# Second down projection of a two-layer decoder: 512 weight columns per matmul in three of four accumulator banks

## The chip, the cores and the metric

The kernel runs on one core of a Trainium2 chip. Its engines are named in the profile as PE (TensorE, the matmuls), PEld (the weight loads of TensorE), DVE (VectorE), ACT (ScalarE), POOL (GpSimd) and SP (SyncE, which issues most of the DMAs). The metric is the device time of one execution in microseconds (us); lower is better. The table below gives the median of three runs.

## The reference

The reference is a decoder trunk of two layers for 256 tokens of 1024 features, all in float32. A layer is a mixer (a gated short convolution in the first layer, causal attention in the second) and a channel mixer, and a last norm follows. The part that matters here is the channel mixer of the second layer and the norm behind it:

```python
def conv_glu_ffn(h, w_up, conv_w, conv_b, w_down):
    u = causal_dwconv(h @ w_up, conv_w) + conv_b
    g, v = jnp.split(u, 2, axis=-1)
    return (jax.nn.silu(g) * v) @ w_down
...
x = x + conv_glu_ffn(rms_norm(x, f_norm[layer]), f_w_up[layer], f_conv[layer],
                     f_conv_b[layer], f_w_down[layer])
return rms_norm(x, final_norm)
```

The hidden size of the channel mixer is 2816, so `w_up` is 1024 x 5632 and `w_down` is 2816 x 1024.

## The kernel before

**Products in three parts.** TensorE works on the type float32r. To keep float32's precision, each operand is split into a high part (written by ScalarE as float32r) and a low part (the rest, by VectorE), and a product is the sum of three matmuls: high by high, high by low, low by high. `mm3` (lines 168 to 171) and `token_bank` (lines 190 to 203) issue these three into the same place of PSUM.

**Units.** The weights come in units, in two sizes. A unit of the big tag B is 128 x 2048 (one block of 128 hidden features of `w_up`, gate and value), a unit of the small tag S is 128 x 1024 (128 rows of `w_down`, for instance). Each tag has three slots. For a unit, SyncE loads the raw tile (`load`), ScalarE makes the high part (`split_hi`, line 91), VectorE the low part (`split_lo`, line 97). A unit knows its place in the list of its tag, `u.at` (line 70). In the S list stand 8 units of `w_mb`, 8 of `w_mo`, 22 of the first `w_down`, 8 of `w_o` and then the 22 of the second `w_down`, `DN[1]`, whose places are therefore 46 to 67. A slot's raw tile is loaded anew when its low part has been made (lines 116 and 117); its high part is rewritten when the unit that held the slot has been marked used.

**The channel mixer.** `ffn` runs over 22 blocks of hidden features, by hand in program order (the schedule is manual: each engine executes its instructions in the order in which they are written). For block i it issues `up_step` (48 matmuls: 8 feature tiles, gate and value, 3 products, each 256 columns for the 256 tokens; the weights of the unit are the stationary operand), `conv` (VectorE and ScalarE: scale, convolution over three tokens; it also calls for the next B splits), `gate` (ScalarE's silu, VectorE's product, then the hidden block split into `sh` and `sl`), and, three blocks behind, the down projection of block i - 3 (`down_step`, lines 205 to 209). The last three down units follow behind the loop in `token_last` (lines 220 to 231), in an order by bank, so that the sums, the norm and the output of one bank can run beside the products of the next.

**The second down projection.** In the second layer, `down_step` calls `token_bank`: there the hidden block is the stationary operand (128 hidden features by 128 tokens, taken from `sh` and `sl`) and the weights of the unit stream by as columns. The result is 256 tokens by 1024 features, in four PSUM banks of 128 tokens by 512 features: bank b has tokens `b // 2` and features `b % 2`. Each bank is filled in two halves of 256 columns (`HALVES`, line 55). Bank 3 has its second half in a bank of its own, `acc[4]` (the tile named misc in the profile), which the end of the kernel needs. One `down_step` is thus 4 banks x 2 halves x 3 products = 24 matmuls of 256 columns, and it adds to what the earlier units have left in the banks; only the first unit's first matmul into a bank has `start`.

**Places in memory.** Many tiles are made wider than needed and start at an offset (64 or 48 elements, for instance lines 84, 139 and 251 to 253). `Rows` (lines 247 to 256) holds the normed input of a stage as 8 tiles of 256 tokens and, in `again`, a second copy of the first one, which stands at 32 elements where the eight stand at 48 + 256 and on. Steps called with `again=True` read this copy for their tile 0; in the second `ffn` these are the steps of blocks 1, 2 and 6.

Of the kernel before, what the change touches and what calls it, by code (L numbers as in the profile page):

```python
# [42 lines left out]
def yoco_kernel(ctx: ExitStack, tc: tile.TileContext, t: dict, out: bass.AP):  # L43
    nc = tc.nc
    V, A, G, PE = nc.vector, nc.scalar, nc.gpsimd, nc.tensor
# [97 lines left out]
    first = const.tile([128, 1], F32, name="first")  # L143
# [43 lines left out]
            mm3(acc[b][:, m % 2, :], u.hi[:, m * 128:(m + 1) * 128], u.lo[:, m * 128:(m + 1) * 128],  # L187
                hh, hl, start=(first and m % 2 == 0), stop=last)

    def token_bank(u, b, acc, hh, hl, first, last, c=slice(0, 512)):  # L190


        tok, f0 = slice(b // 2 * 128, b // 2 * 128 + 128), b % 2 * 512
        for d in HALVES:
            if not c.start <= d.start < c.stop:
                continue
            apart = b == 3 and d.start > 0
            o = acc[4 if apart else b].rearrange("p a s -> p (a s)")[:, d]
            f = slice(f0 + d.start, f0 + d.stop)
            PE.matmul(o, hh[:, tok], u.hi[:, f], start=(first and (apart or d.start == 0)), stop=False,  # L200
                      skip_group_check=True)
            PE.matmul(o, hh[:, tok], u.lo[:, f], start=False, stop=False, skip_group_check=True)  # L202
            PE.matmul(o, hl[:, tok], u.hi[:, f], start=False, stop=last, skip_group_check=True)  # L203
# [16 lines left out]
    def token_last(us, acc, hs):  # L220

        for u in us:
            assert u.lo is not None
        for n, u in enumerate(us):
            for b in (0, 1):
                token_bank(u, b, acc, *hs[n], False, n == len(us) - 1)
        for b, c in ((2, slice(0, 512)), (3, HALVES[0]), (3, HALVES[1])):
            for n, u in enumerate(us):
                token_bank(u, b, acc, *hs[n], False, n == len(us) - 1, c)
        for u in us:  # L230
            u.used = True

    def acc_bank():
        return psum.tile([128, 2, S], F32, name="acc", bufs=4)
# [193 lines left out]
    def mixer_a(j, fill=None):  # L428

        w = [par(P_CONV, 3 * j + n) for n in range(3)]  # L430
        m = tmp.tile([128, 2, S], F32, name="u", bufs=2)
        V.tensor_mul(m[:, 1, :], mc[j][:, 0, :], rr[:, 1, :])
        V.tensor_mul(m[:, 0, :], mc[j][:, 1, :], m[:, 1, :])
        o = tmp.tile([128, 2, S], F32, name="cv", bufs=2)
        A.activation(o[:, 0, :], m[:, 0, :], AF.Identity, scale=w[2])
        hi("B")
        if fill:
            lo(fill)
        tap(o[:, 0, :], m[:, 0, :], w[1], 1)
        tap(o[:, 0, :], m[:, 0, :], w[0], 2)  # L440
        V.tensor_mul(o[:, 1, :], o[:, 0, :], rr[:, 0, :])
        return o[:, 1, :]
# [33 lines left out]
    for i in range(2):  # L476
        o = mixer_a(i, "B")
# [8 lines left out]
    o = mixer_a(3, "B")  # L486
    hi("S")
    mixer_b(3, o, "S")
    acc = [acc_bank() for _ in range(4)]
# [4 lines left out]
    for j in range(4, KT):  # L494
        mc[j] = up_bank()
        up_step(MC[j], mc[j], xh, xl, 2)
        o = mixer_a(j, "S")
# [19 lines left out]
    def ffn(layer, xh, xl, sq, bank=down_bank, between=None):  # L517
# [79 lines left out]
        if bank is token_bank:  # L597
            token_last(dn[FJ - 3:], acc, [hd[j] for j in range(FJ - 3, FJ)])
        else:
            down_step(dn[FJ - 3], acc, hd[FJ - 3])  # L600
            down_last(dn[FJ - 2:], acc, [hd[FJ - 2], hd[FJ - 1]])
# [3 lines left out]
    acc = ffn(0, xh, xl, sq)  # L605
# [274 lines left out]
    acc = [acc_bank() for _ in range(4)]  # L880
# [24 lines left out]
    def turn(n):  # L905
# [5 lines left out]
        V.transpose(dst[:, :, :, 32 * a:32 * a + 32], src)  # L911

    acc = ffn(1, xh, xl, sq, token_bank, turn)


# [102 lines left out]
```

## Time and profile before

| | us |
|---|---|
| median of 3 runs (lowest, highest) | 568.54 (568.38, 568.77) |
| span of the profiled execution | 566.6 |
| busy: PEld / DVE / ACT | 554.1 / 472.9 / 341.7 |
| second up and down projections, first to last matmul | 379.9 to 560.5 |

A profiled execution is one run; its span reaches from the first to the last instruction, and what the runs count beyond it is launch and end. In the timeline rows that follow, the columns are the start (us from the span's start), the duration (us), the engine, the line of the kernel, the operation, the tiles (out<-in) and the shape (rows * columns of the stationary operand, then rows x streamed columns), and xN counts merged neighbours. TensorE's matmuls overlap in these rows, each being shown until its last result is written; what one costs is read from start to start.

### The profile page before, as it was taken

How to read it: one execution, taken by the hardware profiler on the slowest of the kernel's cores; microseconds unless marked ns; L12 is line 12 of the kernel's file. 1: busy time of each engine (PE TensorE's matmuls, PEld its weight loads, DVE VectorE, ACT ScalarE, POOL GpSimd, SP SyncE). 2: the span in 40 equal slices, each digit the busy share in tenths (PEclk: the TensorE clock that was granted, in tenths of full speed). 3: DMA queues.
4: the chain of work that ended last, by engine and by line, in shares of the span. 5: the costliest groups of instructions: out<-in, count | busy, mean ns of one | idle time of the engine just before them, and what ended most of it. 6: DMA issues, size and time to landing. Idle time of an engine off the chain costs nothing.

```text
span 566.6 us, 11823 instructions
## 1 busy us (share of the span) xinstructions
PE 558.4 (99%) x4908; PEld 554.1 (98%) x4908; DVE 472.9 (83%) x817; ACT 341.7 (60%) x525; POOL 10.4 (2%) x32
## 2 busy tenths in 40 slices
PE   8999999999999999999999999999999999999995
PEld 8999999999999999999999999999999999999995
DVE  5998869899877787787897999858999888889876
ACT  7765437567654665466756777656676556546534
POOL 0400000000000000000000000000000000000001
PEclk9999999999999999999999999999999999999998
DMA  8986583447556545655265565644656554563211
GB/s 294 387 300 220 181 299 120 149 152 243 193 197 224 186 160 213 223 175 197 75 214 168 202 206 216 195 178 150 223 186 223 223 193 159 208 222 117 72 38 75
DMA packets 24181, 108.48 MB, mean 191 GB/s; under 512 B 2736, under 2 KB 5440, under 8 KB 16192
## 3 DMA queue, kind: packets, MB, share of 16 engines
q1 hardware_dynamic: 23840, 107.43, 52.9%
q8 instruction: 38, 0.62, 0.4%
q10 hardware_dynamic: 288, 0.30, 0.1%
q14 instruction: 15, 0.12, 0.1%
HBM read 106.65 MB, written 1.07 MB: 190 GB/s over the span
## 4 chain that ended last, share of the span: by engine, by line
PE 97%; DMA 1%; ACT 1%; issue 0%; DVE 0%; SPq 0%; POOLq 0%; POOL 0%; ACTq 0%
PE up L171 20%; PE up L169 20%; PE up L170 20%; PE acc L169 7%; PE acc L171 7%; PE acc L170 7%; PE acc L203 3%; PE acc L200 3%; PE acc L202 3%; PE up L757 1%; PE acc L627 1%; PE acc L629 1%; PE acc L630 1%; DMA xres<-xT 1%; PE acc L682 1%; PE misc L203 0%
## 5 line engine op out<-in xcount | busy, mean ns | idle before, releaser
L169 PE MATMUL up<-xh,hiB 128*128 128x256 f32 x944 | 261.4, 277 | 0.8 <-ACT hiB L91 0.8
L171 PE MATMUL up<-xh,loB 128*128 128x256 f32 x944 | 261.1, 277 | 0.3 <-DVE loB L97 0.2
L170 PE MATMUL up<-xl,hiB 128*128 128x256 f32 x944 | 260.8, 276 | 0.0
L169 PEld LDWEIGHTS up<-xh,hiB 128*128 128x128 f32 x944 | 177.2, 188 | 1.5 <-ACT hiB L91 1.0
L171 PEld LDWEIGHTS up<-xh,loB 128*128 128x128 f32 x944 | 177.2, 188 | 0.7 <-DVE loB L97 0.7
L170 PEld LDWEIGHTS up<-xl,hiB 128*128 128x128 f32 x944 | 177.3, 188 | 0.0
L97 DVE TENSOR_TENSOR loB<-rawB,hiB 128x2048 fp32r<-128x2048 f32 (+2 forms) x76 | 147.8, 1948 | 3.7 <-ACT hiB L91 3.5
L91 ACT ACTIVATE hiB<-rawB 128x2048 fp32r<-128x2048 f32 (+1 forms) x73 | 123.6, 1697 | 15.2 <-PE up L170 7.0
L532 ACT ACTIVATE cv<-u,pk 128x256 f32<-128x256 f32 x88 | 48.2, 595 | 69.3 <-DVE u L525 69.3
L97 DVE TENSOR_TENSOR loS<-rawS,hiS 128x1024 fp32r<-128x1024 f32 (+2 forms) x73 | 83.5, 1147 | 6.4 <-ACT hiS L91 6.0
L397 DVE SCALAR_TENSOR_TENSOR cv<-u,pk,cv 128x255 f32<-128x255 f32 x192 | 81.4, 479 | 2.7 <-ACT cv L532 1.7
L91 ACT ACTIVATE hiS<-rawS 128x1024 fp32r<-128x1024 f32 (+2 forms) x73 | 72.0, 987 | 8.9 <-PE acc L170 5.3
L525 DVE TENSOR_TENSOR u<-up,rr 128x512 f32<-128x512 f32 x44 | 30.3, 688 | 44.9 <-PE up L171 43.0
L171 PE MATMUL acc<-sh,loS 128*128 128x256 f32 x240 | 66.2, 276 | 0.0
L169 PE MATMUL acc<-sh,hiS 128*128 128x256 f32 x240 | 66.2, 276 | 0.0
L170 PE MATMUL acc<-sl,hiS 128*128 128x256 f32 x240 | 66.2, 276 | 0.0
L394 ACT ACTIVATE sh<-hid 128x256 fp32r<-128x256 f32 x52 | 21.7, 417 | 58.5 <-DVE hid L549 53.7
L171 PEld LDWEIGHTS acc<-sh,loS 128*128 128x128 f32 x240 | 45.1, 188 | 0.0
L169 PEld LDWEIGHTS acc<-sh,hiS 128*128 128x128 f32 x240 | 45.1, 188 | 0.0
L170 PEld LDWEIGHTS acc<-sl,hiS 128*128 128x128 f32 x240 | 45.0, 188 | 0.0
L200 PE MATMUL acc<-hiS,sh 128*128 128x256 f32 x154 | 42.5, 276 | 0.0
L202 PE MATMUL acc<-loS,sh 128*128 128x256 f32 x154 | 42.5, 276 | 0.0
(180 smaller groups left out, 780.3 us busy)
## 6 DMA issues: line engine op xcount, KB each, us to landing
rawB<-w_up SPq DMA_DIRECT2D x44, 1024.0 KB, 4.7
rawS<-w_dn SPq DMA_DIRECT2D x44, 512.0 KB, 3.4
rawB<-w_qk SPq DMA_DIRECT2D x8, 1024.0 KB, 4.8
rawB<-w_mc SPq DMA_DIRECT2D x6, 1024.0 KB, 8.1
rawS<-w_mo SPq DMA_DIRECT2D x8, 512.0 KB, 5.1
rawB<-w_v SPq DMA_DIRECT2D x4, 1024.0 KB, 4.7
rawS<-w_o SPq DMA_DIRECT2D x8, 512.0 KB, 4.0
rawS<-w_mb SPq DMA_DIRECT2D x7, 512.0 KB, 5.7
```

What stands on the lines that cost most here:

```text
L91: A.activation(self.hi[:, c], self.raw[:, c], AF.Copy)
L97: V.tensor_sub(self.lo[:, c], self.raw[:, c], f32(self.hi[:, c]))
L169: PE.matmul(o, wh, xh, start=start, stop=False, skip_group_check=True)
L170: PE.matmul(o, wh, xl, start=False, stop=False, skip_group_check=True)
L171: PE.matmul(o, wl, xh, start=False, stop=stop, skip_group_check=True)
L200: PE.matmul(o, hh[:, tok], u.hi[:, f], start=(first and (apart or d.start == 0)), stop=False, skip_group_check=True)
L202: PE.matmul(o, hh[:, tok], u.lo[:, f], start=False, stop=False, skip_group_check=True)
L203: PE.matmul(o, hl[:, tok], u.hi[:, f], start=False, stop=last, skip_group_check=True)
L394: return (h, lw), lambda: A.activation(h, src, AF.Copy), lambda: V.tensor_sub(lw, src, f32(h))
L397: V.scalar_tensor_tensor(o[:, back:], u[:, :S - back], w, o[:, back:], op0=OP.mult, op1=OP.add)
L525: V.tensor_mul(u, ub[j], rr[:, 0:1, :].to_broadcast([128, 2, S]))
L532: A.activation(o[:, half, :], u[:, half, :], AF.Identity, scale=cw[half][2], bias=par(P_FCB, c0 + half * FJ))
```

## The change

`token_bank` gets a branch. For banks 0 to 2, where the call asks for the whole bank and is not one of `token_last`, each of the three products is one matmul with 512 columns in place of two with 256. In units with an odd place in the S list the columns are taken in another order: 16 of the first half, 16 of the second half, 16 of the first, and so on, the same in the weights and in the bank. Bank 3 and the last three units are computed as before.

```diff
-    def token_bank(u, b, acc, hh, hl, first, last, c=slice(0, 512)):
+    def token_bank(u, b, acc, hh, hl, first, last, c=slice(0, 512), ending=False):
         tok, f0 = slice(b // 2 * 128, b // 2 * 128 + 128), b % 2 * 512
+        if not last and b < 3 and c.stop == 512 and not ending:
+            turns = u.at % 2 == 1
+
+            def run(a):
+                return a.rearrange("p (h k i) -> p k h i", h=2, i=16) if turns else a
+
+            o = run(acc[b].rearrange("p a s -> p (a s)"))
+            wh, wl = run(u.hi[:, f0:f0 + 512]), run(u.lo[:, f0:f0 + 512])
+            PE.matmul(o, hh[:, tok], wh, start=first, stop=False, skip_group_check=True)
+            PE.matmul(o, hh[:, tok], wl, start=False, stop=False, skip_group_check=True)
+            PE.matmul(o, hl[:, tok], wh, start=False, stop=False, skip_group_check=True)
+            return
         for d in HALVES:
...
             for b in (0, 1):
-                token_bank(u, b, acc, *hs[n], False, n == len(us) - 1)
+                token_bank(u, b, acc, *hs[n], False, n == len(us) - 1, ending=True)
         for b, c in ((2, slice(0, 512)), (3, HALVES[0]), (3, HALVES[1])):
             for n, u in enumerate(us):
-                token_bank(u, b, acc, *hs[n], False, n == len(us) - 1, c)
+                token_bank(u, b, acc, *hs[n], False, n == len(us) - 1, c, True)
```

## The prediction

> **What bounds the kernel now.** I read the page first: the span, the busy shares, the slices, the chain of work.
>
> ```profile
> span 566.6 us, 11823 instructions
> PE 558.4 (99%) x4908; PEld 554.1 (98%) x4908; DVE 472.9 (83%) x817; ACT 341.7 (60%) x525; POOL 10.4 (2%) x32
> PEclk9999999999999999999999999999999999999998
> PE 97%; DMA 1%; ACT 1%; issue 0%; DVE 0%; SPq 0%; POOLq 0%; POOL 0%; ACTq 0%
> ```
>
> The chain lies on TensorE for 97%, at the full granted clock until the last slice. So a change to TensorE's instructions comes through one for one as long as nothing else becomes late. The question is what one matmul costs. The timeline around one step of the second down projection (columns: start, duration, engine, line) tells it:
>
> ```profile
> 500.51 0.28 PE L200 MATMUL acc<-hiS,sh 128*128 128x256 f32 x1
> ...
> 501.07 0.28 PE L203 MATMUL acc<-hiS,sl 128*128 128x256 f32 x1
> 501.08 0.19 PEld L200 LDWEIGHTS acc<-hiS,sh 128*128 128x128 f32 x1
> 501.19 0.28 PE L200 MATMUL acc<-hiS,sh 128*128 128x256 f32 x1
> 501.19 0.19 PEld L202 LDWEIGHTS acc<-loS,sh 128*128 128x128 f32 x1
> 501.30 0.28 PE L202 MATMUL acc<-loS,sh 128*128 128x256 f32 x1
> ...
> 503.23 0.28 PE L169 MATMUL up<-xh,hiB 128*128 128x256 f32 x1
> ```
>
> The durations overlap; only starts count. The step has 4 banks by 2 halves by 3 products, 24 matmuls, from 500.51 to 503.23: 2.72 us, 113.3 ns each. Each load starts with the matmul before it (501.08 after 501.07), and its own matmul starts 0.11 us after the load. This looks like a chain of loads: load, switch, next load. Or it could be the stream of 256 columns that takes 113 ns. Two other places separate the two readings:
>
> ```profile
> 317.83 0.27 PE L682 MATMUL misc<-u 64*128 64x128 f32 x1
> ...
> 317.94 0.27 PE L682 MATMUL misc<-u 64*128 64x128 f32 x1
> ...
> 319.29 0.39 PE L757 MATMUL up<-pT,vs 128*64 128x256 f32 x2
> 319.50 0.39 PE L757 MATMUL up<-late,vs 128*64 128x128 f32 x4
> ...
> 387.29 0.53 PEld L342 LDWEIGHTS misc<-ones,sq 128*128 128x128 f32 x4
> 387.40 0.50 PE L342 MATMUL misc<-ones,sq 128*128 128x1 f32 x4
> ```
>
> The L342 matmuls stream a single column. Yet their four loads cover 0.53 us; less the 0.19 of the last one that is 0.34 for three, 113 ns per load with nothing to stream. L757 and L682 are the opposite, smaller loads under fp32 streams: after 256 columns the next starts 0.21 us later, after 128 columns 0.11. An fp32 column must be about as long as two fp32r columns, since 256 of those fit into 0.113. So I read: a stream of 256 fp32r columns takes some 0.108, one of 512 some 0.215, and what sets 113.3 now is the load.
>
> Do the other engines leave room? Windows over one period (PE, PEld, DVE, ACT, POOL busy) and the waits from 402 to 549 us:
>
> ```profile
> 500.51:508.67 8.16, 8.16 (x75) 8.16 (x73) 6.97 (x10) 4.61 (x6) 0.00 (x0) 1.00 0.54 194
> DVE u L525 <- PE up L171: 14.9, 13, 1.2
> ```
>
> VectorE works 6.97 of 8.16 us and waits for TensorE at L525 in 13 periods. ScalarE has more room, the DMA engines are at 0.54.
>
> **The change part by part.** How many matmuls are merged: the view of line L202 counts the middle product.
>
> ```profile
> L202 PE MATMUL acc<-loS,sh x154: 276/276/276, 402.7 to 559.1; 128*128 128x256 f32 x154
> L202 PE MATMUL misc<-loS,sh x22: 276/276/276, 405.0 to 560.1; 128*128 128x256 f32 x22
> ```
>
> 154 + 22 = 176 = 22 units by 8 half banks. The last three units go through token_last with ending set and stay as they are. In 19 units, banks 0 to 2 turn six matmuls of 256 columns into three of 512: 9 merged per unit, 171 in all, with 171 loads and 171 matmuls fewer. Bank 3 keeps its six.
>
> Price of a merged matmul. No row shows 512 columns of fp32r. The nearest is L757's 256 of fp32, a stream with its load hidden, at 0.21 (rounded; 0.205 to 0.22). The next load starts with the merged matmul and is ready 0.11 us later, 0.10 us before it is wanted. Bounds: 0.212 if only the columns count (twice 0.106, the half of L757's step); 0.220 if each matmul has a fixed cost of some 7 ns beside its columns (0.1133 + 0.106, rounded up); 0.2267 if the stream itself takes 113.3 per 256 columns, which is no gain. I take 0.216, the middle of the first two, because L342 shows the load alone at 113. Gain per merged matmul: 0.2267 - 0.216 = 10.7 ns; 171 x 10.7 = **1.83 us**. At the bounds: 2.5, 1.15 and 0 us.
>
> The interleaved order (units whose place in the S list is odd: DN[1] starts at 46, so 9 of the 19) reads 16 columns of the first half, 16 of the second, and writes the bank in the same order. No matmul of this trace reads or writes in such runs. Below: nothing, since each run is whole and contiguous, so 0.216 as well; 1.83 holds. Above, from the nearest rows, the step of up unit 6 that uses the shifted copy `again` (it stands 64 bytes off the others' 128-byte rhythm, lines 252 and 253):
>
> ```profile
> 425.66 0.28 PE L169 MATMUL up<-xh,hiB 128*128 128x256 f32 x1
> ...
> 426.38 0.28 PE L169 MATMUL up<-xh,hiB 128*128 128x256 f32 x1
> ```
>
> Six matmuls in 0.72 us, 0.120 each: another place in memory costs 6 to 7 ns per 256 columns. Two such lengths would make 0.240; then the 81 interleaved ones lose 81 x 13 ns = 1.08 us and the 90 plain ones win 0.96, nothing in sum. I take the lower end, and keep this end for the range. The Trainium skill, SBUF — State Buffer, section "Door 1: The DMA port swizzle", says that reads are free as long as they use a 16-byte line more than once; runs of 64 bytes satisfy that, and no run here shows it. Its rule for writes speaks the other way and is a rival below.
>
> What becomes late next. The units' loads and splits have slack in steady state: VectorE's idle time per period, 8.16 - 6.97 = 1.19 us, shrinks by 9 x 10.7 = 0.096. But at the start of the stage VectorE is behind. TensorE needs loB of the sixth up unit there, and two merged steps come ahead of it:
>
> ```profile
> 411.11 2.28 DVE L97 TENSOR_TENSOR loB<-rawB,hiB 128x2048 fp32r<-128x2048 f32 x1
> 413.54 0.19 PEld L171 LDWEIGHTS up<-xh,loB 128*128 128x128 f32 x1
> 8.17 0.69 DVE L97 TENSOR_TENSOR loB<-rawB,hiB 128x512 fp32r<-128x512 f32 x1
> 8.91 0.19 PEld L171 LDWEIGHTS up<-xh,loB 128*128 128x128 f32 x1 [0.31 <-DVE loB L97]
> ```
>
> loB is ready at 413.39. From a real wait (8.86 to 8.91) a load follows 0.05 later, so 413.44 at the earliest. TensorE would come at 413.54 - 2 x 0.096 = 413.35. It waits 0.09 us, and behind this load on TensorE's queue stands the whole up step; nothing else waits for it, as VectorE's chain there is paced by itself. I subtract 0.1. No wait is added by the code, and no DMA moves: the units are marked used at the end of the step as before, so loads are asked for at most 1.8 us earlier at the end of the stage.
>
> The end of the kernel (last products, sums, output) keeps its matmuls; it follows bank by bank and moves forward whole.
>
> Sum: 1.83 - 0.10 = 1.73 us. The profiled execution's span of 566.6 becomes 564.9. The 1.9 us between that span and the median of 568.54 lie outside it and stay: 568.54 - 1.73 = **566.8 us**, -0.30%.
>
> **The rivals.** (1) *The pace slips.* The same 256-column matmuls have a second pace in this trace. After the stall at L342:
>
> ```profile
> 387.96 0.28 PE L170 MATMUL up<-xl,hiB 128*128 128x256 f32 x1
> ...
> 389.73 0.28 PE L170 MATMUL up<-xl,hiB 128*128 128x256 f32 x1
> 389.85 0.28 PE L171 MATMUL up<-xh,loB 128*128 128x256 f32 x1
> 389.97 0.29 PE L169 MATMUL up<-xh,hiB 128*128 128x256 f32 x1
> ...
> 391.05 0.28 PE L169 MATMUL up<-xh,hiB 128*128 128x256 f32 x1
> ...
> 391.95 0.28 PE L171 MATMUL up<-xh,loB 128*128 128x256 f32 x1
> ```
>
> Fifteen in 1.77 us, 118 ns each, by operands that run at 113 elsewhere and at the same granted clock. From 389.97 the step with the shifted copy follows (six), and from 391.05 on it is eight in 0.90 us, 113 again. So two streams, the load's and the columns', can lock in a worse rhythm. If a merged matmul knocks them into it, the rest of the period pays: bank 3's 6 and the 48 of the up step, 54 x 4.5 ns = 0.24 us against 0.096 won. In all 19 periods: +0.147 x 19 = +2.8 us, **571.3 us**. It decides from 0.096/0.24, two periods in five; in every second one (one of the two orders only) the sum is about +0.5 us, 569.0. For it: behind the first merged matmul, a step with the shifted copy stands once only (up unit 6), so nothing else repairs it. Against it: in the stage itself all steps keep 113.3, and each merged matmul starts its next load at the same distance as now.
>
> (2) *The interleaved order costs.* Each merged one of that order has 32 runs. If each run cost 1 ns more, 81 x 32 = 2.6 us against 1.73 won: 569.4; at 2 ns 572.0. It turns slower than before at 0.7 ns per run. Nothing in the profile has such a write, for or against. The Trainium skill, PSUM — Partial Sum Buffer, section "Specifications (TRN2)", states that any non-contiguous pattern slows matmuls significantly, by 8-byte lines. By that rule this case comes true; no run here shows it, and runs of 64 bytes fill their lines.
>
> (3) *The stream, not the load, takes 113.3.* Then nothing is won: 568.5. Against it stands L342. With the fixed cost of 6.7 ns instead (0.220), 1.15 - 0.1 gives 567.5.
>
> **How the numbers follow.** Forecast (0.212 to 0.218 per merged matmul, both orders, no slip; 566.1 to 567.2): 0.57. Fixed cost or part of the meeting price (567.2 to 568.3): 0.13. No gain at all (568.5): 0.07. Slip or runs in about half of the units (568.6 to 569.6): 0.08. Slip throughout: 0.09. Runs dear: 0.06. A measurement here can tell about 0.2%, 1.1 us. Faster by more than that (under 567.4): 0.58, a little of the second case with the first. Slower (over 569.7): the last two, 0.15. Within: the rest, 0.27. The range takes in the first four cases up to half of the fourth: 566.1 to 569.1, 0.81.
>
> **What would show it.** In the changed trace: matmuls of 128x512, 9 per unit, 57 of each product, starting 0.216 apart, with the load 0.10 ahead of need; steps of 2.62 us in place of 2.72, in plain and interleaved units alike; up steps still 5.44; one wait of about 0.1 for loB near 413.4; L525's wait shorter by 0.1 per period. Up steps of 5.65 would show rival 1; merged matmuls of the odd units longer than those of the even ones, rival 2; merged at 0.227, rival 3. I would be wrong if the load is not what sets 113.3, or if a long matmul disturbs its neighbours.

## The result, and the profile after

The changed kernel is slower: 572.93 us (median of 4 runs, 572.16 to 573.18) against 568.65 us (4 runs, 568.38 to 569.05) of the kernel before, a ratio of 1.0071 with the interval 1.0057 to 1.0085. The interval lies above 1, and the time above the range of the prediction. The page of the changed kernel begins so (span, busy times, the granted clock in 40 slices, the chain of work by engine):

```profile
span 570.4 us, 11481 instructions
PE 563.2 (99%) x4737; PEld 550.9 (97%) x4737; DVE 472.8 (83%) x817; ACT 341.7 (60%) x525; POOL 10.3 (2%) x32
PEclk9999999999999999999999999999999999999999
PE 97%; ACT 1%; DMA 1%; issue 0%; DVE 0%; POOLq 0%; POOL 0%; ACTq 0%
```

The 171 matmuls are gone (4908 to 4737), the clock is full, the chain still lies on TensorE for 97%. So TensorE does the same products with fewer instructions in more time; busy shares can't tell why. The timeline of one plain step and of the interleaved one after it does, by its starts (lines 202 to 204 are the merged products, 212 to 215 those of bank 3):

```profile
402.19 0.39 PE L202 MATMUL acc<-hiS,sh 128*128 128x512 f32 x1
402.42 0.40 PE L203 MATMUL acc<-loS,sh 128*128 128x512 f32 x1
402.65 0.39 PE L204 MATMUL acc<-hiS,sl 128*128 128x512 f32 x1
...
404.28 0.28 PE L212 MATMUL acc<-hiS,sh 128*128 128x256 f32 x1
...
404.99 0.28 PE L169 MATMUL up<-xh,hiB 128*128 128x256 f32 x1
...
410.64 0.40 PE L202 MATMUL acc<-hiS,sh 128*128 128x512 f32 x1
410.88 0.40 PE L203 MATMUL acc<-loS,sh 128*128 128x512 f32 x1
...
412.80 0.28 PE L212 MATMUL acc<-hiS,sh 128*128 128x256 f32 x1
...
413.50 0.28 PE L169 MATMUL up<-xh,hiB 128*128 128x256 f32 x1
```

Nine merged matmuls take 2.09 us in the plain step (404.28 - 402.19) and 2.16 in the interleaved one, 0.232 and 0.240 each. Two matmuls of 256 columns took 0.2267. To the nanosecond, the starts of the plain nine lie 226, 236, 231, 235, 231, 236, 231, 236 and 231 apart; the interleaved nine lie 240 apart throughout. None is under 225.

The second loss shows in a table of windows over the next periods (columns: length, then busy time and instructions of PE, PEld, DVE, ACT and POOL, granted clock, DMA share, GB/s): merged products, bank 3 and up step of a plain unit, then of an interleaved one.

```profile
435.69:437.78 2.09, 2.09 (x11) 1.69 (x10) 1.89 (x3) 1.17 (x3) 0.00 (x0) 1.00 0.53 210
437.78:438.49 0.71, 0.71 (x8) 0.71 (x6) 0.71 (x1) 0.71 (x1) 0.00 (x0) 1.00 0.08 23
438.49:444.14 5.65, 5.65 (x50) 5.65 (x49) 4.37 (x8) 2.74 (x4) 0.00 (x0) 1.00 0.69 250
444.14:446.30 2.16, 2.16 (x11) 1.73 (x10) 1.96 (x3) 1.23 (x3) 0.00 (x0) 1.00 0.18 74
446.30:447.00 0.70, 0.70 (x8) 0.69 (x7) 0.70 (x1) 0.70 (x1) 0.00 (x0) 1.00 0.00 0
447.00:452.44 5.44, 5.44 (x51) 5.44 (x50) 4.32 (x8) 2.68 (x4) 0.00 (x0) 1.00 0.70 234
```

PE is busy without a hole in every row and the clock is 1.00. Yet the up step behind a plain unit takes 5.65 us, 117.8 ns per matmul, and the one behind an interleaved unit 5.44, 113.3 ns, with the same 48 matmuls on operands of the same kind. A period is 8.45 us behind a plain unit and 8.29 behind an interleaved one; before, all were 8.16, but for one with the shifted copy in its up step (8.21).

The account, from start to start (steps before: 2.040 for what is now merged, 0.680 for bank 3, 5.440 for the up step): a plain period loses 0.052 + 0.027 + 0.213 = 0.29 us, an interleaved one 0.121 + 0.013 = 0.13. Nine of each, 402.189 to 552.915, are 150.73 us; the same 18 took 146.93 before (402.541 to 549.468): +3.80. From there to the end of the span it is 17.45 against 17.14, +0.32: the last of these units is plain, and `token_last` follows at 118 ns. The profiled execution had been 0.35 ahead when the stage began, where the kernels do not differ. 3.80 + 0.32 - 0.35 = 3.77, the difference of the spans to within 0.01 (570.37 - 566.61).

VectorE only waits for it. In the views of waits over the same steps (402 to 549 us before, 402 to 552 now), its wait for the up step's last product was 14.9 us and is now 3.8 longer:

```profile
DVE u L537 <- PE up L171: 18.7, 14, 1.5
```

### The profile page after: what moved, and what is told of

Its sections match the earlier page's. It is cut to its first block, busy times and chain, and to the rows that moved or that the text cites. A ratio compares the mean times of both kernels' runs of the same rounds, so it can differ in the third digit from the quotient of the medians.

```text
span 570.4 us, 11481 instructions
## 1 busy us (share of the span) xinstructions
PE 563.2 (99%) x4737; PEld 550.9 (97%) x4737; DVE 472.8 (83%) x817; ACT 341.7 (60%) x525; POOL 10.3 (2%) x32
## 4 chain that ended last, share of the span: by engine, by line
PE 97%; ACT 1%; DMA 1%; issue 0%; DVE 0%; POOLq 0%; POOL 0%; ACTq 0%
PE up L169 20%; PE up L171 20%; PE up L170 20%; PE acc L169 7%; PE acc L171 7%; PE acc L170 7%; PE acc L203 2%; PE acc L204 2%; PE acc L202 2%; PE up L769 1%; PE acc L639 1%; PE acc L641 1%; PE acc L642 1%; PE acc L212 1%; PE acc L694 1%; PE acc L214 1%
## 5 line engine op out<-in xcount | busy, mean ns | idle before, releaser
L295 ACT ACTIVATE xh<-xres,pk 128x256 fp32r<-128x256 f32 x40 | 17.8, 498 | 11.9 <-DVE xres L322 9.3
L555 ACT ACTIVATE sl<-cv 128x256 f32<-128x256 f32 x44 | 18.3, 417 | 8.2 <-DVE cv L409 8.1
```

Of the source, the lines that this page charges most:

```text
L295: A.activation(xh[:, k, :], order(x[:, k, :]), AF.Identity, scale=par(gain, k))
L555: A.activation(sl, o[:, 0, :], AF.Silu)
```

## The experiments

Three things were open: why a merged matmul is not shorter than two, whether it is the plain order that slows what follows, and what the interleaved order does. The diffs are against the changed kernel. The numbers of single matmuls are start to start from the trace. A time given without a range is that of one run.

### All units plain, all units interleaved

```diff
-            turns = u.at % 2 == 1
+            turns = False
```

> All 19 units merge banks 0 to 2 in plain order (no unit takes 16 columns from each half in turn). In the changed kernel a plain step leaves the pace of the 256-column matmuls at 117.8 ns and an interleaved one brings it back to 113.3. Theory P (a plain merged matmul is what slips the pace, and only the interleaved order repairs it): every up step behind the first takes 5.65 us, except that the step with the shifted copy in up unit 6 may end at 113.3; merged matmuls 231 to 236 ns, step plus up step 8.46 us against 8.16; 19 periods and the tail then come to about +5.5 us, 574 us. Rival Q (the pace only alternates with the number of merged matmuls, whatever their order): up steps alternate 5.65 and 5.44 as in the changed kernel, about 572 us.

572.36 us (572.04 to 573.06), ratio 1.0071 (1.0054 to 1.0087). Windows of two merged runs, each followed by its up step:

```profile
436.33:438.43 2.10, 2.10 (x12) 1.70 (x10) 1.90 (x3) 1.17 (x3) 0.00 (x0) 1.00 0.45 179
439.11:444.55 5.44, 5.44 (x50) 5.44 (x49) 4.40 (x8) 2.76 (x4) 0.00 (x0) 1.00 0.61 230
444.55:446.64 2.09, 2.09 (x11) 1.70 (x10) 1.89 (x3) 1.16 (x3) 0.00 (x0) 1.00 0.38 153
447.35:453.00 5.65, 5.65 (x50) 5.65 (x49) 4.38 (x8) 2.74 (x4) 0.00 (x0) 1.00 0.68 246
```

All units are now plain, and still only every second up step is slow, with one exception: the step of up unit 6 is slow until it reads the shifted copy, runs at 113 ns behind that, and so the next unit too is entered at the fast pace and leaves the slow one. A plain unit entered at the fast pace begins with 226, 236 and leaves the slow one behind; entered at the slow pace it begins with 231, 229 and leaves the fast one. So the plain unit flips the pace both ways. The slow pace is not a lasting damage that only the interleaved order would repair.

```diff
-            turns = u.at % 2 == 1
+            turns = True
```

> All 19 units merge banks 0 to 2 in the interleaved order. Theory P (interleaved matmuls cost 240 ns each but leave the pace at 113.3): merged 0.240 each, every up step 5.44 us, step plus up step 8.30 against 8.16; 19 x 0.134 = +2.5 us, about 571.2 us. Rival Q (the pace alternates): up steps of 5.65 in every second period, 573 us or more. Rival R (240 is what an interleaved matmul costs only when it meets the slow pace, and about 226 at the fast one): 569 us.

571.34 us (570.98 to 571.64), ratio 1.0048 (1.0033 to 1.0063). Merged products and up step of one unit (the first window begins a little before its nine and shows 2.17 for 2.161):

```profile
444.76:446.93 2.17, 2.17 (x12) 1.73 (x11) 1.97 (x3) 1.24 (x3) 0.00 (x0) 1.00 0.25 102
447.62:453.06 5.44, 5.44 (x51) 5.44 (x49) 4.32 (x8) 2.69 (x4) 0.00 (x0) 1.00 0.68 245
```

Each interleaved matmul takes 240 ns, each up step 5.440 (5.487 with the shifted copy, as before the change): the interleaved order leaves the fast pace behind and pays for it in its own matmuls. 19 x 0.134 = 2.5 us of loss against 2.66 of the medians (571.34 - 568.68).

### Is it the stream: other widths, another type

```diff
-            PE.matmul(o, hh[:, tok], wh, start=first, stop=False, skip_group_check=True)
...
+            for d in (slice(0, 384), slice(384, 512)):
+                o = acc[b].rearrange("p a s -> p (a s)")[:, d]
+                f = slice(f0 + d.start, f0 + d.stop)
...
```

The columns of a bank go as 384 and 128, three products each, in plain order.

> Each product of banks 0 to 2 is one matmul of 384 and one of 128 columns, instead of one of 512; same columns, plain order. It measures what a stream of each length costs with one load each. Theory S (the stream sets the pace, 113.3 per 256 columns in proportion; a load takes less): 384 columns 170 ns at the fast pace (175 at the slow one), 128 columns 57 or whatever the load alone needs. My forecast's theory L (the load needs 113 and hides shorter streams; streams cost 0.417 ns per column and a few ns): 384 columns 163 ns, 128 columns 113. A fixed 6.7 ns per matmul: 384 columns 167.

578.71 us. The timeline of six matmuls, and behind it that of the loads beside the last of them:

```profile
446.14 0.33 PE L198 MATMUL acc<-hiS,sh 128*128 128x384 f32 x1
446.31 0.34 PE L200 MATMUL acc<-loS,sh 128*128 128x384 f32 x1
446.49 0.34 PE L201 MATMUL acc<-hiS,sl 128*128 128x384 f32 x1
446.66 0.22 PE L198 MATMUL acc<-hiS,sh 128*128 128x128 f32 x1
446.72 0.28 PE L200 MATMUL acc<-loS,sh 128*128 128x128 f32 x1
446.83 0.28 PE L201 MATMUL acc<-hiS,sl 128*128 128x128 f32 x1
```

```profile
446.77 0.19 PEld L201 LDWEIGHTS acc<-hiS,sl 128*128 128x128 f32 x1
446.88 0.19 PEld L198 LDWEIGHTS acc<-hiS,sh 128*128 128x128 f32 x1
446.99 0.19 PEld L200 LDWEIGHTS acc<-loS,sh 128*128 128x128 f32 x1
```

384 columns take 0.17 to 0.18 (0.52 for three), not the 0.163 that the prediction's column would give: 1.5 times 113.3 is 170. The 128-column matmuls follow each other at 0.11, because their loads do (446.77, .88, .99). Where a load is late, the matmul is shown from before its load starts (446.72 and 446.77), so single steps shift: the first 128 columns show 0.06, and the 384 columns behind the last ones, not printed here, 0.23. Over a whole unit, with bank 3 at its old 0.680, a pair of 384 and 128 takes 0.287, which is about 0.173 and 0.113. So both things are there, a load of about 0.11 and a stream of 113.3 per 256 columns or a little more, and at 256 columns they are equally long.

```diff
+    wb = wide.bitcast(mybir.dt.bfloat16)
+    xb = wb[:, 32:160]
...
+            for n in range(3):
+                PE.matmul(o, xb, wb, start=(first and n == 0), stop=False, skip_group_check=True)
```

> The merged matmuls of banks 0 to 2 read a constant bf16 tile (512 columns of 2 bytes, and 128 bf16 columns as the stationary operand) in place of the split weights and the hidden block, so the down projection of 19 units is left out except for bank 3. It halves the bytes of the stream and of the load with the same 512 columns. Theory S1 (the stream is held at 113.3 per 256 columns by its 4 bytes per column): 216 ns or less per merged matmul, and the pace behind it stays at 113.3 or not, as it falls. Theory S2 (512 columns cost 226 and more whatever their bytes, by the writing of the bank or a fixed cost): 226 to 236 ns.

567.18 us, 1.5 below the kernel before on the same chip. The nine merged matmuls of a unit, as one row:

```profile
410.65 2.12 PE L200 MATMUL acc<-ones 128*128 128x512 bf16 x9
```

Eight steps and the 0.38 of the last matmul are 2.12: the first step takes 226, each further one 215 to 216. This is the price that the prediction used, and the kernel gains with it; only it belongs to narrower elements that lie side by side. The Trainium skill, TensorE: Matmul & The Clock Gate, section "Back-to-back issue gap", has a formula for the isolated gap from one matmul to the next at full clock, and the estimate by it is 215.8 ns for 512 columns; it agrees with these 216 and not with the 226 and more of the type used here. This run also shows the late low part. VectorE's split and TensorE's load behind it:

```profile
411.11 2.28 DVE L97 TENSOR_TENSOR loB<-rawB,hiB 128x2048 fp32r<-128x2048 f32 x1
413.45 0.19 PEld L174 LDWEIGHTS up<-xh,loB 128*128 128x128 f32 x1
```

The split ends at 413.39, the load starts 0.06 later, 142 ns behind the load before it, and its own matmul takes 149 ns in place of 113.

Next, the kernel's own numbers, cut down to bf16 by reading the upper two bytes of each element where it stands, at every fourth byte:

```diff
+            def upper(a):
+                return a.bitcast(mybir.dt.bfloat16).rearrange("p (n two) -> p n two", two=2)[:, :, 1]
...
+            wh, wl = upper(u.hi[:, f0:f0 + 512]), upper(u.lo[:, f0:f0 + 512])
+            PE.matmul(o, upper(hh[:, tok]), wh, start=first, stop=False, skip_group_check=True)
```

> The merged matmuls of all 19 units read the upper two bytes of every weight and of every hidden value as bf16 (so the products of banks 0 to 2 are computed in bf16): 512 columns in steps of 4 bytes, at the same places as with float32r. Theory Y1 (float32r itself streams at 17/16 of a column's time, and loads slowly): 216 ns per merged matmul, as with the narrow bf16 tile. Theory Y2 (a rate of reading memory, 64 bytes in 17 column times, whatever the type): 226 ns or more.

569.29 us beside 568.98 of the kernel before. Matmuls, then their loads:

```profile
444.84 0.39 PE L202 MATMUL acc<-loS,sh 128*128 128x512 bf16 x1
445.06 0.39 PE L203 MATMUL acc<-hiS,sl 128*128 128x512 bf16 x1
445.29 0.39 PE L201 MATMUL acc<-hiS,sh 128*128 128x512 bf16 x1
445.52 0.39 PE L202 MATMUL acc<-loS,sh 128*128 128x512 bf16 x1
```

```profile
444.84 0.10 PEld L203 LDWEIGHTS <-sl 128*128 128x128 bf16 x1
445.06 0.10 PEld L201 LDWEIGHTS <-sh 128*128 128x128 bf16 x1
```

225 to 227 each, but for the first of the nine, which takes 239 where the trace has it. The type is that of the run before and the load is as short (0.10, where a float32r load lasts 0.19), and yet the time is the least that float32r takes. What differs from the 216 is that the elements stand four bytes apart, and are the kernel's data in the kernel's tiles rather than one constant. With these short loads there is no 231 and no 236.

### Which side of the interleaved order costs, and what is read

Reading interleaved and writing plain, then the reverse.

```diff
-            o = run(acc[b].rearrange("p a s -> p (a s)"))
+            o = acc[b].rearrange("p a s -> p (a s)")
```

> All 19 units: the weights are read by 16 columns from each half in turn, the bank is written in plain order (so the columns of banks 0 to 2 come out in another order than the reference's). Theory V (the 240 ns and the repair of the pace come from the order of reading): 240 ns per merged matmul, up steps 5.44, as with both orders interleaved. Rival W (they come from writing the bank in runs): 231 to 236 ns, up steps alternating 5.65 and 5.44, as with the plain order.

```diff
-            wh, wl = run(u.hi[:, f0:f0 + 512]), run(u.lo[:, f0:f0 + 512])
+            wh, wl = u.hi[:, f0:f0 + 512], u.lo[:, f0:f0 + 512]
```

> All 19 units: the weights are read in plain order, the bank is written by 16 columns to each half in turn (so the columns of banks 0 to 2 come out in another order than the reference's). Theory V: 231 to 236 ns and alternating up steps, as with the plain order. Rival W: 240 ns, up steps 5.44.

571.53 and 571.70 us. First the windows of the reading one (merged, up step), then of the writing one (merged, up step, next merged):

```profile
444.66:446.82 2.16, 2.16 (x11) 1.72 (x10) 1.96 (x3) 1.23 (x3) 0.00 (x0) 1.00 0.26 106
447.51:452.95 5.44, 5.44 (x50) 5.44 (x49) 4.33 (x8) 2.69 (x4) 0.00 (x0) 1.00 0.67 247
```

```profile
444.19:446.28 2.09, 2.09 (x11) 1.70 (x10) 1.89 (x3) 1.16 (x3) 0.00 (x0) 1.00 0.30 123
446.99:452.64 5.65, 5.65 (x50) 5.65 (x49) 4.38 (x8) 2.74 (x4) 0.00 (x0) 1.00 0.70 249
452.64:454.74 2.10, 2.10 (x12) 1.70 (x10) 1.90 (x3) 1.17 (x3) 0.00 (x0) 1.00 0.19 78
```

The reading order brings the whole of it: 2.16 and 5.44 as with both sides interleaved. Writing in 32 runs of 64 bytes gives 226, 236, 231 and the up steps of 5.65 and 5.44 in turn, as in the kernel that is all plain. So the writes cost nothing here, against the rule of the Trainium skill, PSUM — Partial Sum Buffer, section "Specifications (TRN2)", that the prediction weighed.

All 512 columns from a single run of 64 bytes, read 32 times:

```diff
+            def line(a):
+                return a[:, f0:f0 + 16].rearrange("p (k i) -> p k i", k=1).to_broadcast([128, 32, 16])
...
+            wh, wl = line(u.hi), line(u.lo)
```

> All 19 units: each merged matmul of 512 columns reads the same 16 weight columns 32 times (so banks 0 to 2 hold another product than the reference's); reads stay in one run of 64 bytes. Theory X (a column of 4 bytes costs 17/16 of a column's time because new 64-byte runs have to be fetched, beside the load's): 216 ns per merged matmul, as with bf16. Rival Y (float32r streams at 17/16 whatever it reads): 226 ns or more.

571.17 us:

```profile
444.35:446.50 2.15, 2.15 (x12) 1.70 (x11) 1.95 (x3) 1.22 (x3) 0.00 (x0) 1.00 0.24 95
```

225 ns for the third and the seventh of the nine, 238 to 244 for the others. Reading the same bytes again is not faster; 225 is the least here too.

The weights 64 bytes (16 elements) further forward in their tile, all units plain:

```diff
-    DN[1] = [Unit(t["w_dn"][1, i], SMALL, at=192) for i in range(FJ)]
+    DN[1] = [Unit(t["w_dn"][1, i], SMALL, at=128) for i in range(FJ)]
```

> All 19 units merged in plain order, and the weights of the second down projection stand 64 bytes earlier in their tiles (at=128 in place of 192), so that they lie in the rhythm of the shifted copy towards the hidden block. Theory T (what a merged matmul costs above 226.7 comes from where its stream and the next load meet; the floor of 226.7 from the stream itself): the cost moves to other values, none under 226; bank 3's 256-column matmuls go to about 119 ns as in the step with the shifted copy; the pace behind the step may or may not flip. Rival (the 231 to 236 are a fixed cost of 512 columns): 231 to 236 again.

570.86 us beside 568.98. Merged products and up step:

```profile
444.18:446.28 2.10, 2.10 (x11) 1.69 (x10) 1.90 (x3) 1.17 (x3) 0.00 (x0) 1.00 0.28 111
446.99:452.44 5.45, 5.45 (x50) 5.45 (x49) 4.37 (x8) 2.73 (x4) 0.00 (x0) 1.00 0.66 245
```

The nine now take 237 to 238 and 229 to 230 in turn, 234 on the mean; bank 3's matmuls take 117 on the mean, where 119 was expected. Every up step is near the fast pace (5.452): in this place nine plain matmuls leave no slow pace behind. The place moves what stands above 226 about; it brings none under it.

### An even number of plain ones, and shorter loads

```diff
-        if not last and b < 3 and c.stop == 512 and not ending:
-            turns = u.at % 2 == 1
+        if not last and b < 2 and c.stop == 512 and not ending:
+            turns = False
```

Six merged matmuls per unit, all plain; banks 2 and 3 in halves.

> Banks 0 and 1 alone are merged, in plain order, in all 19 units: six merged matmuls per unit in place of nine. Theory T (a plain merged matmul flips the pace of what follows between 113.3 and 117.8, so an odd number per unit leaves it flipped and an even number restores it): merged 226, 236, 231, 236, 231, 236 ns, together 1.40 us against 1.36, and every up step at 5.44; 19 x 0.04 = +0.8 us, about 569.5 us. Rival U (nine flips by accident; any plain merged matmul may leave the slow pace): up steps of 5.65 in half of the periods or more, 571 us and over.

569.39 us (10 runs, 569.03 to 569.92), ratio 1.0012 (1.0002 to 1.0022). Merged, the twelve of banks 2 and 3, up step:

```profile
443.81:445.20 1.39, 1.39 (x8) 1.13 (x7) 1.19 (x3) 0.47 (x1) 0.00 (x0) 1.00 0.44 180
445.20:446.57 1.37, 1.37 (x14) 1.36 (x12) 1.37 (x1) 1.37 (x3) 0.00 (x0) 1.00 0.00 0
446.57:452.01 5.44, 5.44 (x51) 5.44 (x49) 4.42 (x8) 2.78 (x4) 0.00 (x0) 1.00 0.65 245
```

226, 236, 231, 235, 231, 236, then one of 118, and 113 to the end. So six plain ones give the pace back where nine flip it. That each of them flips it fits both; other numbers were not run, and it holds for this place of the weights only (see the run before). The loss is what six matmuls cost too much: 6 x 5.8 + 5 = 40 ns in 19 units, 0.76 us, against 0.63 measured.

The second and third product with 64 of the 128 tokens only, all plain, so that two of three loads have half the columns (and two of three products write half the partitions):

```diff
+            PE.matmul(o[0:64, :], hh[:, t0:t0 + 64], wl, start=False, stop=False, skip_group_check=True)
+            PE.matmul(o[0:64, :], hl[:, t0:t0 + 64], wh, start=False, stop=False, skip_group_check=True)
```

> All 171 merged products in plain order; the first of three (hi tokens by hi weights) loads all 128 tokens, the other two only 64 of them (tokens 64 to 127 of the lo products of banks 0 to 2 are left out in the 19 units), so that their loads are half as long. While a product of 512 columns runs, the load of the next one runs beside it: beside the first and the second the load is a half one, beside the third a full one. Theory M (what stands over 226 ns in the plain order, 231 and 236, is time that the stream loses where it meets the next load): products beside a half load take 226 to 231, those beside a full load 231 to 236, nine take about 2.06 us. Theory F (a 512-column product costs its 231 to 236 by its own start or address): nine take 2.09 as in the kernel with all products plain, whatever the load. Theory L of the prediction (the load sets the pace) would give less than 226 for the products whose next load is short; expected not to be seen. Time by M 571 to 572, by F 572.4, with up steps of 5.65 in some or all units, since the flip of the pace is not touched.

569.32 us beside 568.84:

```profile
443.63 0.39 PE L198 MATMUL acc<-hiS,sh 128*128 128x512 f32 x1
443.86 0.40 PE L199 MATMUL acc<-loS,sh 128*64 128x512 f32 x1
444.10 0.40 PE L200 MATMUL acc<-hiS,sl 128*64 128x512 f32 x1
```

226, 234, 235, 229, 233, 233, 227, 235 and 231. In the trace the loads of 64 columns last 0.13 to 0.14 us in place of 0.19, so they are shorter, but not by half. Theory M does not hold as it was put: the second of each three runs beside a short load and takes 232 to 235. Nor does F: nine take 2.083 us rather than 2.09, and, with nine in a unit as before, no up step is slow, so that the 571 us and more of both theories did not come. So the shorter loads, or the half outputs that came with them, have a part in the flip of the pace, and what exactly stands above 226 stays open.

No version with float32r beat the kernel before, and nothing in these runs points to a gain by this way: the least that 512 columns of this type took in any run is 225 ns, at most 1.7 less than two matmuls of 256, and the mean of nine was never under 231.

## Why the prediction was wrong

**What bounds the kernel.** TensorE, at full clock, a change comes through one for one: right. The loss of the spans, 3.8 us, is the loss of TensorE's steps.

**The price of a merged matmul is the step that failed.** "I take 0.216 ... because L342 shows the load alone at 113". L342 does show a load of about 0.11 (of float32 there), and the 128-column matmuls of float32r show it again. But that a load takes 0.11 says nothing on whether the stream of 256 columns takes less. The other leg, L757's 0.21 for 256 columns of fp32 halved to 0.106, carried a length across types: a float32r stream takes 170 ns and more at 384 columns and 225 and more at 512, that is 113 per 256 or a little more, where elements two bytes apart give 216 at 512. Nor was that 0.21 the step of a single matmul: L757's rows come in pairs (the x2 and x4), two matmuls on 64 columns of the stationary operand starting 7 ns apart (319.288 and 319.295) and the next two 0.209 later. Load and stream are equally long at 256 columns; taking one load away leaves the stream. This is the prediction's third rival, to which it gave 0.07 because L342 stood "against it"; L342 was no evidence against it. Of the gain of 1.83 us nothing came.

**Plain merged matmuls, mean 232.5 ns.** This cost was not priced: it lies above the bound of 0.2267, by 5.8 ns each, 90 x 5.8 = 0.52 us.

**The interleaved order.** The upper bound, two steps of the shifted copy, 0.240, met the measured 240 ns. That the reads cost and not the writes is shown: turning only the reads gave the 240, only the writes nothing. That the same thing slows the shifted copy and these reads is not, so the equal number may be luck. The lower end was taken, on the ground that each run is whole and contiguous; the reads were slower none the less. The 81 matmuls cost 81 x 13.4 = 1.09 us, the loss worked out there. The rival of dear writes fell.

**The pace.** The first rival had its price right (0.24 us in bank 3 and the up step; measured 0.027 + 0.213), and also its form "in every second one". The argument against it, that each merged matmul starts its next load at the same distance as now, was the wrong test: the next load still does, and the pace slips none the less. The loads behind the first two matmuls of the plain step (402.19 and 402.42) show it:

```profile
402.19 0.19 PEld L203 LDWEIGHTS acc<-loS,sh 128*128 128x128 f32 x1
402.42 0.19 PEld L204 LDWEIGHTS acc<-hiS,sl 128*128 128x128 f32 x1
```

The rival's time for this case, 569.0, came too low because it still counted the 1.83 us as won and no loss in the merged matmuls themselves. Its rows hold one slip of reading: from 389.97 to 391.05 stand nine steps, the six with the shifted copy and three behind them at 116 to 123 ns. The step with the shifted copy does lead from the slow pace to the fast one there, as it does in the kernel that is all plain. With the slip behind nine units, their bank 3, the small steps behind the interleaved ones and the end (9 x 0.24 + 9 x 0.013 + 0.34; the last is bank 3 and 71 matmuls of `token_last` at 4.5 ns more) it cost 2.62 us.

0.52 + 1.09 + 2.62 = 4.2, where the medians differ by 4.28.

**The rest.** The counts held (57 of each product). The wait for loB did not arise, since TensorE came later rather than earlier; where merged matmuls were short (the bf16 constant) it arose at the place named, 0.06 behind the split's end, at some 0.04 in place of 0.09 us. The up steps of 5.65 that the prediction named as the sign of the first rival stand in the trace.

## What to carry to other kernels

That one of two overlapped parts takes as long as the whole step does not show that the other is shorter; measure the other by itself (here one run with another width would have done) before pricing its removal. Don't carry a stream's length from one type to another. Where matmuls are packed without a hole, look at how the steps behind a change run, not at the changed ones alone: more than half of this loss lay in instructions that were not touched.

## What the runs showed of the hardware

- 512 columns read at two bytes each from contiguous memory took 216 ns, the same type read at every fourth byte 225 to 227, float32r 225 and more. The loads were as short (0.10 us) in both bf16 runs. So the longer time goes with the distance of the elements rather than with the type or the load; but the two bf16 runs also differ in their data and their tiles, and no run separates these from the distance.
- The same 256-column matmuls run at 113.3 or 117.8 ns with no wait, at the full clock. Nine plain 512-column matmuls before them flip the one into the other, six leave it as it was, and nine interleaved ones lead to the fast one. With the weights 64 bytes elsewhere, or with loads of 64 columns for two of three products, nine plain ones left no slow pace behind. That the two paces are two ways in which the reads of stream and load meet in memory fits all of this, the shifted copy and the moved weights too, but it was only argued.
- Writing a bank in runs of 64 bytes took the same time as in order (2.09 and 2.10 us for nine).
